# The mixer of a gated decoder step, in another order

## The chip, the cores and the metric

The kernel runs on one core of one Trainium2 chip, as a single launch. The metric is the device time of an execution in microseconds (us). Three runs of the kernel before took 2404.18, 2404.9 and 2407.2 us; the median is 2404.9.

## The reference, cut to what matters

All arithmetic is float32. One layer works on 304 token columns: 16 meta tokens, 256 prompt tokens, and 8 samples of 4 new tokens.

```
x = x + 1/2 * SwiGLU_1(rms(x))
z = rms(x) @ W_in                      # 2048 -> 1024 + 1024 + 2048 + 2048 columns
u_pool, u_ssm, g_a, g_b = z
a = pool_mix(u_pool)                   # window means (2, 4, 8, 16) less u, then a 256x256 map per group, a scale
s = gelu(s5_scan(u_ssm))               # complex diagonal recurrence over the tokens, 64 groups of 64 states
s = s * sigmoid(s @ W_glu + b_glu)
x = x + (sigmoid(g_a + b) * (a @ W_a) + sigmoid(g_b + b) * (s @ W_b)) @ W_out
x = x + 1/2 * SwiGLU_2(rms(x))
y = rms(x)                             # and the new histories and scan states are returned
```

The gates, the branches and everything after them need only the 288 columns without the meta tokens.

## The kernel before, in words

**Layout.** Features lie on the partitions, tokens along the free dimension. Every float32 matrix product is made of three products of float32r parts: high times high, high times low, low times high (`mm3`, L241 to L245).

**Weights.** All weights are read once, in chunks of 512 x 256 (512 KB), in the order that `weight_order` writes out: 698 chunks. For each chunk SP issues a load into one of three `raw` buffers (`load`), ScalarE makes the high part `whi` (L143) and VectorE the low part `wlo` (L152), which frees the raw buffer. Both parts have four buffers and run two chunks ahead of their use. A chunk is 24 matmuls.

**Projections.** `proj` multiplies two column tiles of a weight with the activations, into two of four PSUM banks. After each chunk it calls `step`. A step emits, in this order: the high part of a later chunk, the functions that wait in `g.post` (they read the banks of the projection before), the low part of that chunk, the next load, and then pieces of side work: `g.side` is one generator of which `g.rate` pieces are taken per step on average. The order of the instructions on each engine's queue is that in which they are emitted.

**Mixer.** The first projection `ps0` of the combined input weight is made before `mixer` begins. Then follow, in this order: three more projections for the pool columns, four for the ssm columns, eight times a gate-a projection and a branch-a projection (after the first gate `mixed()` makes the per-group pool maps, on the same four banks), eight gate-b projections, and, once `drain` has emptied the side work, the GLU and branch b.

**Side work.** While the first ssm projections run, the pool branch is the side work, 3.5 pieces per step (`Pool.run`, 40 pieces for four groups; the first piece of a group reads the projection's two banks, L971). At the first ssm projection it is drained, and the scan takes its place after a lag of 7 steps, 2.35 pieces per step. The scan (`Scan.run`) goes through 16 batches. A batch has 12 vector steps (`rows`, L887 to L897, two of them scan instructions), six products with the input (`into`, L835, whose results ScalarE copies) and the products with the output matrix (`outof`, L846). For each batch `load` issues four kinds of DMA on POOL's queue: u, expanded in DRAM (`stk`, 228 KB), the input matrices `bl` (384 KB), the turning factors `ee` (912 KB), and u itself for every other one.

**u of the scan.** `u_in` takes a tile of the ssm columns from its bank, splits it in two parts, stores it once from SP (`usc`) and three times from POOL (`stk`, L1035, 152 KB each).

**Gates.** `gate` multiplies a bank by 1/rms (L1041) and takes the sigmoid; a gates are multiplied with branch a and stored (`msc`), b gates are stored (`gsc`), from SP.

Of the kernel before, what the change touches and what calls it, by code (L numbers as in the profile page):

```python
# [36 lines left out]
MIXRATE = 2.35  # L37
# [5 lines left out]
JB = 2  # L43
NA = S0 // 16
NTV = 16 + NA
POOLRATE = 3.5
LATE = 8
LAG = 7
# [35 lines left out]
def weight_order():  # L84
    """Every weight chunk in the order of use: (array, first row tile, row tiles, first column)."""
    def cols(name, c0, kd):
        return [(name, k0, KC, c0) for k0 in range(0, kd, KC)]

    def ffn_order(i):
        out = []  # L90
        down = lambda c: [(f"ffn{i}_w_down", c * FC, FC, q * 256) for q in range(8)]
        for p in range(NF // 2):
            out += cols(f"ffn{i}_w_gate", p * 256, KD) + cols(f"ffn{i}_w_up", p * 256, KD)
            if p >= 3 and p % 2 == 1:
                out += down((p - 3) // 2)
        return out + down(NF // FC - 1)

    out = ffn_order(1)
    for p in range(KW):
        out += cols("w_in", p * 256, KD)  # L100
    for p in range(KD // 2):
        out += cols("w_in", 2 * WP + p * 256, KD)
        if p == 0:
            out += [("pool_w", 0, 4, 0), ("pool_w", 4, 4, 0)]
        out += cols("w_branch_a", p * 256, KW)
    for p in range(KD // 2):
        out += cols("w_in", 2 * WP + D + p * 256, KD)
    for p in range(KW // 2):
        out += cols("glu_w", p * 256, KW)
    for p in range(KD // 2):  # L110
        out += cols("w_branch_b", p * 256, KW)
    for p in range(KD // 2):
        out += cols("w_out", p * 256, KD)
    return out + ffn_order(2)


class Weights:
    """Brings the chunks in ahead of their use and splits each in two float32r parts."""
# [44 lines left out]
def setup(ctx, tc, I):  # L163
    g = Ctx()
    nc = tc.nc
    g.tc, g.nc, g.I = tc, nc, I
    g.uid = 0
    g.side, g.rate, g.owed, g.post = None, 0, 0.0, []
    g.dram = ctx.enter_context(tc.tile_pool(name="dram", bufs=1, space=DRAM))
    g.const = ctx.enter_context(tc.tile_pool(name="const", bufs=1))  # L170
    g.w = Weights(g, ctx.enter_context(tc.tile_pool(name="wpool", bufs=2)))
    g.act = ctx.enter_context(tc.tile_pool(name="act", bufs=1))
    g.parts = {"X": (g.act, 2 * KD)}
    g.psum = ctx.enter_context(tc.tile_pool(name="psum", bufs=4, space=PSUM))
    g.psaux = ctx.enter_context(tc.tile_pool(name="psaux", bufs=3, space=PSUM))
    g.pslong = ctx.enter_context(tc.tile_pool(name="pslong", bufs=1, space=PSUM))
    g.downs = 0

    g.ident = g.const.tile([P, P], F32, name="ident")
    make_identity(nc, g.ident)  # L180
    g.ones = g.const.tile([P, P], F32, name="ones")
    nc.vector.memset(g.ones, 1.0)
    g.vec = g.const.tile([P, 120], F32, name="vec")
    g.hc = g.const.tile([P, NT + NTV + 2], F32, name="hc")
    g.isc = g.dram.tile([32, JB, NT], F32R, name="isc")
    return g


def load_vectors(g, pool):
    """The per-feature vectors as columns; the first of them is wanted before the others."""  # L190
    nc, I = g.nc, g.I
    vr = pool.tile([P, P], F32, name="vr")
    for name, (r0, n) in VROWS.items():
        src = I[name] if name == "final_norm" else I[name][0]
        nc.gpsimd.dma_start(vr[r0:r0 + n], src.rearrange("(k p) -> k p", p=P))
    nc.gpsimd.dma_start(g.hc, I["consts"])

    def turn(r0, n):
        ps = bank(g, "vt", aux=True)
        nc.tensor.transpose(ps[:, :n], vr[:n], g.ident[:n, :n])  # L200
        nc.vector.tensor_copy(g.vec[:, r0:n], ps[:, r0:n])

    return turn
# [7 lines left out]
def step(g):  # L211
    """Closes a chunk of products: what waits for the chunk before it, then some of the side work."""
    g.w.high()
    flush(g)
    g.w.low()
    g.w.load()
    g.owed += g.rate
    while g.owed >= 1.0:
        g.owed -= 1.0
        got = next(g.side, None) if g.side is not None else None  # L220
        if got is None:
            g.side = None
# [8 lines left out]
def also(g, more):  # L231
    g.side = more if g.side is None else chain(g.side, more)


def drain(g):
    while g.side is not None:
        if next(g.side, None) is None:
            g.side = None
# [9 lines left out]
def warm(g, func):  # L248
    """Has the function's table loaded before it is needed."""
    t = g.act.tile([P, 1], F32, tag="warm", name=nm(g, "warm"))  # L250
    g.nc.scalar.activation(t, g.ones[:, :1], func)
# [11 lines left out]
def split(g, src, n, which, scale=None):  # L263
    """src (times a per-row scale) as two float32r parts whose sum it is."""
# [21 lines left out]
class Norm:  # L286
    """x * gain goes on in two parts; the token's 1/rms is applied to the products (add),
    or to x itself (scaled) once every row tile has been seen by square."""
# [9 lines left out]
    def add(self, xts, squares=True, late=None):  # L298
        """The next row tiles of x; their low parts wait in late if it is given."""
# [35 lines left out]
    def inverse(self):  # L335
        """1/rms of each token as a column of a small tile, from the sums of its squares."""
# [20 lines left out]
    def spread(self):  # L357
        """1/rms of each token in a bank, the same in every row."""
# [11 lines left out]
def rsqrt(g, y, src, shape):  # L370
    """1 / sqrt(src / D + EPS): a guess from the bits, negated, and three Newton steps that each flip it."""
# [14 lines left out]
def load_x(g, tp, norm):  # L386
    """Pieces of the token rows, turned so that features lie on partitions; also their squares' sums."""
# [39 lines left out]
def proj(g, name, c0, xs, n, kd, before=None):  # L427
    """The products of two 128-column tiles of a weight from column c0 on with xs; each in a bank."""
# [14 lines left out]
def ffn(g, pool, norm, i, hpart, done, before=None, last=False):  # L443
    """x += 0.5 * (silu(xn wg) * (xn wu)) wd; done(ms) once row tiles ms of x are whole."""
# [93 lines left out]
def ssm_setup(g):  # L538
    """Everything of the scan that its inputs do not touch; yields between pieces."""
# [261 lines left out]
class Scan:  # L801
    """The groups' states in a frame that turns with them, so that the scan's factors are real."""

    def __init__(self, g, sp, usc, stk):
# [6 lines left out]
        self.yps = {}  # L811
# [3 lines left out]

    def load(self, sb):
        g, sp, nc = self.g, self.sp, self.g.nc
        i, half = divmod(sb, 4 // JB)
        ee = sp.tile([P, 3, JB, NT], F32, tag="ee", name=nm(g, "ee"), bufs=2)
        bl = sp.tile([P, 3 * JB, P], F32R, tag="bl", name=nm(g, "bl"), bufs=1)  # L820
        nc.gpsimd.dma_start(self.stk[sb % 2][:96], self.up[i][half * JB:(half + 1) * JB].rearrange("j r t -> r j t"))
        nc.gpsimd.dma_start(bl, g.bsc[sb])
        nc.gpsimd.dma_start(ee, g.esc[sb])
# [5 lines left out]
    def into(self, sb, s, k):  # L829
        """One of the products with the input that the next batch starts from."""  # L830
# [32 lines left out]
    def rows(self, sb, s):  # L863
        """The batch's work, one vector instruction at a time."""
# [35 lines left out]
    def run(self):  # L900
        nb = NJ // JB
        nxt = self.load(0)
        yield 1
        yield 1
# [39 lines left out]
class Pool:  # L944
    """The pooling branch: each tile's window means less itself, and the new history."""
# [19 lines left out]
    def run(self, p, pss, norm, out):  # L965
        """The group's work, in pieces."""
        g, nc, n = self.g, self.g.nc, NB * HIST
        if norm.r is None:
            norm.finish()
# [46 lines left out]
def mixer(g, norm, O, ps0):  # L1016
    """Gated sum of the two branches; returns its row tiles in two parts."""
# [27 lines left out]
    with ExitStack() as cm:  # L1045
        g.mix = cm.enter_context(g.tc.tile_pool(name="mix", bufs=1))
        with ExitStack() as cs:
# [5 lines left out]
            g.side, g.rate = None, POOLRATE  # L1053
            for p in range(KW // 2):
                pool.fetch(p)
                ps = proj(g, "w_in", p * 256, norm.x, NT, KD) if p else ps0
                more = lambda p=p, ps=ps: also(g, pool.run(p, ps, norm, dparts))
                g.post.append(more if p else lambda more=more: g.post.append(more))
            nc.gpsimd.dma_start(O[3][0, :, :HIST - NS], g.I["state_pool"][0, :, NS:])
            for p in range(KW // 2):  # L1060
                ps = proj(g, "w_in", WP + p * 256, norm.x, NT, KD)
                g.post += [lambda i=2 * p + f, q=ps[f]: u_in(i, q) for f in range(2)]
                if p == 0:
                    drain(g)
                    g.side, g.rate = scan.run(), MIXRATE
                    g.owed = -LAG * MIXRATE
# [17 lines left out]
            for p in range(KD // 2):  # L1084
                pg = proj(g, "w_in", 2 * WP + p * 256, live, NL, KD)
# [12 lines left out]
            for p in range(KD // 2):  # L1098
                pg = proj(g, "w_in", 2 * WP + D + p * 256, live, NL, KD)

                def gated(p=p, pg=pg):
                    for f in range(2):
                        nc.sync.dma_start(gsc[2 * p + f], gate(pg[f], KD + 2 * p + f))

                g.post.append(gated)
# [3 lines left out]
        g.side, g.rate = scan.store(O, mixb), 0.5  # L1109
# [37 lines left out]
def final(g, ctx, O):  # L1147
    """done(ms) for the last layer, and the closing norm."""
# [67 lines left out]
def body(ctx, tc, I, O):  # L1216
# [6 lines left out]
    with ExitStack() as c1:  # L1223
# [37 lines left out]
        def started():  # L1261
            ct.close()
            g.side, g.rate = ssm_setup(g), SETRATE
# [12 lines left out]
        ps0 = proj(g, "w_in", 0, n2.x, NT, KD, lambda c: [late.pop(0)() for _ in range(min(len(late), 2))])  # L1276
# [52 lines left out]
```

## Time and profile before

The profile is of one execution; its span, from the first to the last instruction, is also its own time as the trace gives it. The runs are timed without it.

| | |
|---|---|
| median of three runs | 2404.9 us |
| profiled execution, span | 2402.5 us |
| TensorE busy | 2368.2 us, 99% of the span |
| VectorE busy | 1593.5 us, 66% |
| ScalarE busy | 1013.3 us, 42% |
| DMA, mean | 185 GB/s |
| mixer, from its first projection to the GLU | about 922 to 1365 us of the span |

Reading it: busy times overlap, so the engine with 99% sets the time, and what the other engines do costs something only where TensorE waits for it. TensorE starts matmuls closer together than one lasts, so their durations add up to more than its busy time. The arrow in a name reads "out <- in".

### The profile page before, as it was taken

To read this page: it belongs to the slowest core of one execution; us is meant where nothing else is said; L and a number is where in the kernel's file an instruction comes from. 1 tells how busy PE (TensorE), PEld (TensorE's weight loads), DVE (VectorE), ACT (ScalarE), POOL (GpSimd) and SP (SyncE) were. 2 spreads that over 40 slices of the span, in tenths; PEclk is the share of its full clock that TensorE was granted. 3 is DMA by queue.
4 is the path that set the end of the run, shared out by engine and by line. 5 is a ranking of instruction groups with operands and counts; after the bars stand their busy time and mean duration, and the time that the engine had idled before them with its cause. 6 is when DMAs were issued, how large, how long until landed. Compare 5 with 4: busy or idle time off the path is not lost.

```text
span 2402.5 us, 42577 instructions
## 1 busy us (share of the span) xinstructions
PE 2368.2 (99%) x17321; PEld 2339.4 (97%) x17321; DVE 1593.5 (66%) x2416; ACT 1013.3 (42%) x1617; POOL 137.6 (6%) x233
## 2 busy tenths in 40 slices
PE   8999999999999999979999999999999999999998
PEld 8999999999999999979999999999999999999997
DVE  6788777876655558669988775555555555555555
ACT  5333333344564335344445444433333333333334
POOL 1000000001110002220101031000000000000000
PEclk9999999999999999989999999999999999999999
DMA  6555666666555556697777576555555555555553
GB/s 195 156 154 188 201 200 197 205 202 180 182 178 181 158 159 197 174 252 236 234 233 245 183 246 208 162 167 167 166 167 164 163 167 166 167 166 168 167 167 110
DMA packets 407076, 443.27 MB, mean 185 GB/s; under 512 B 25036, under 2 KB 393904, under 8 KB 406872
## 3 DMA queue, kind: packets, MB, share of 16 engines
q1 hardware_dynamic: 376512, 376.75, 50.5%
q0 software_dynamic: 30368, 63.80, 9.0%
q8 instruction: 136, 2.23, 0.4%
q14 instruction: 60, 0.49, 0.1%
HBM read 404.30 MB, written 36.51 MB: 183 GB/s over the span
## 4 chain that ended last, share of the span: by engine, by line
PE 89%; issue 6%; DMA 2%; DVE 2%; POOL 1%; ACT 1%; SPq 0%; ACTq 0%; POOLq 0%; DVEq 0%
PE pj L243 21%; PE pj L244 21%; PE pj L245 21%; PE dn L243 7%; PE dn L245 7%; PE dn L244 7%; PE yps L846 1%; DVE wlo L152 1%; DMA bl<-bsc 1%; DMA raw<-in_ffn_w_gate 1%; PE bu L835 1%; POOL bd L756 0%; DMA raw<-in_w_branch_a 0%; ACT whi L143 0%; POOL stk L1035 0%
## 5 line engine op out<-in xcount | busy, mean ns | idle before, releaser
L152 DVE TENSOR_TENSOR wlo<-raw,whi 128x1024 fp32r<-128x1024 f32 x698 | 852.6, 1223 | 596.9 <-ACT whi L143 593.0
L143 ACT CAST whi<-raw 128x1024 fp32r<-128x1024 f32 x698 | 732.9, 1051 | 1102.4 <-PE pj L244 626.8
L243 PE MATMUL pj<-X,whi 128*128 128x304 f32 (+1 forms) x2432 | 739.4, 304 | 0.0
L244 PE MATMUL pj<-X,whi 128*128 128x304 f32 (+1 forms) x2432 | 732.8, 301 | 0.0
L245 PE MATMUL pj<-X,wlo 128*128 128x304 f32 (+1 forms) x2432 | 731.9, 301 | 0.2 <-DVE wlo L152 0.2
L244 PE MATMUL pj<-Y,whi 128*128 128x288 f32 x1728 | 510.8, 296 | 0.0
L243 PE MATMUL pj<-Y,whi 128*128 128x288 f32 x1728 | 510.5, 295 | 0.0
L245 PE MATMUL pj<-Y,wlo 128*128 128x288 f32 x1728 | 509.4, 295 | 0.0
L243 PEld LDWEIGHTS pj<-X,whi 128*128 128x128 f32 x2432 | 459.0, 189 | 6.2 <-issue 5.6
L245 PEld LDWEIGHTS pj<-X,wlo 128*128 128x128 f32 x2432 | 460.0, 189 | 0.6 <-DVE wlo L152 0.6
L244 PEld LDWEIGHTS pj<-X,whi 128*128 128x128 f32 x2432 | 460.3, 189 | 0.0
L243 PEld LDWEIGHTS pj<-Y,whi 128*128 128x128 f32 x1728 | 325.9, 189 | 1.5 <-issue 0.9
L244 PEld LDWEIGHTS pj<-Y,whi 128*128 128x128 f32 x1728 | 325.2, 188 | 0.0
L245 PEld LDWEIGHTS pj<-Y,wlo 128*128 128x128 f32 x1728 | 325.2, 188 | 0.0
L243 PE MATMUL dn<-H,whi 128*128 128x304 f32 x704 | 213.8, 304 | 0.2 <-DVE x L481 0.2
L245 PE MATMUL dn<-H,wlo 128*128 128x304 f32 x704 | 213.2, 303 | 0.0
L244 PE MATMUL dn<-H,whi 128*128 128x304 f32 x704 | 212.4, 302 | 0.0
L244 PE MATMUL dn<-X,whi 128*128 128x288 f32 x704 | 208.1, 296 | 0.0
L243 PE MATMUL dn<-X,whi 128*128 128x288 f32 x704 | 208.1, 296 | 0.0
L245 PE MATMUL dn<-X,wlo 128*128 128x288 f32 x704 | 207.9, 295 | 0.0
L243 PEld LDWEIGHTS dn<-X,whi 128*128 128x128 f32 x704 | 132.9, 189 | 0.0
L243 PEld LDWEIGHTS dn<-H,whi 128*128 128x128 f32 x704 | 132.4, 188 | 0.5 <-DVE x L481 0.5
(274 smaller groups left out, 2009.4 us busy)
## 6 DMA issues: line engine op xcount, KB each, us to landing
raw<-in_ffn_w_gate SPq DMA_DIRECT2D x176, 512.0 KB, 3.6
raw<-in_ffn_w_up SPq DMA_DIRECT2D x176, 512.0 KB, 3.6
raw<-in_ffn_w_down SPq DMA_DIRECT2D x176, 512.0 KB, 3.5
raw<-in_w_in SPq DMA_DIRECT2D x96, 512.0 KB, 4.7
raw<-in_w_out SPq DMA_DIRECT2D x32, 512.0 KB, 4.4
esc<-ee POOLq DMA_DIRECT2D x16, 912.0 KB, 5.0
ee<-esc POOLq DMA_DIRECT2D x16, 912.0 KB, 7.5
raw<-in_w_branch_a SPq DMA_DIRECT2D x16, 512.0 KB, 4.4
```

The costliest lines, as they stand in the source:

```text
L143: self.g.nc.scalar.copy(hi, self.raw[i])
L152: self.g.nc.vector.tensor_tensor(lo, raw, hi.bitcast(F32), ALU.subtract)
L243: mm(ps, wh, x[0], start=start, stop=False)
L244: mm(ps, wh, x[1], start=False, stop=False)
L245: mm(ps, wl, x[0], start=False, stop=stop)
L835: self.g.nc.tensor.matmul(ps, s["bl"][:, jj * 3 + ri], self.stk[sb % 2][:, jj], start=True, stop=True)
L846: g.nc.tensor.matmul(self.yps[i][o:o + 32], g.clhs[h][:, sb * JB + jj], s["k"][h][:, jj, NMETA:], start=k == 0, stop=k == 2)
```

## The change

- The order of the projections becomes: ssm columns (the first of them is now `ps0`), pool columns, the eight gate-b projections, then the eight pairs of gate a and branch a, with `mixed()` after the first gate a. `weight_order` follows.
- The single side work becomes a list of `Lane` objects, each with its generator, its rate and what it is owed; a step takes pieces from each of them in turn. The scan's lane is made after the second ssm projection, with 1.5 pieces per step (`MIXRATE0`) after 5 steps of lag. The pool branch has a lane of its own with 1.8 pieces per step, made when the first pool projection is done, and is extended by each of the others. Once it is empty the scan's lane gets 2.25 pieces per step.
- `Scan.__init__` issues the loads of `bl` for batch 0 and of `ee` for batches 0 and 1; `load` issues those that are not there yet. `load(0)` is called where the lane is made.
- `norm.finish` runs in the step before the first `u_in`, not inside the pool's first piece.
- Docstrings are emptied.

```diff
-MIXRATE = 2.35
+MIXRATE = 2.25
+MIXRATE0 = 1.5
-POOLRATE = 3.5
+POOLRATE = 1.8
-LAG = 7
+LAG = 5
...
 def step(g):
     g.w.high()
     flush(g)
     g.w.low()
     g.w.load()
-    g.owed += g.rate
-    while g.owed >= 1.0:
-        g.owed -= 1.0
-        got = next(g.side, None) if g.side is not None else None
-        if got is None:
-            g.side = None
+    for lane in list(g.lanes):
+        lane.go()
...
+class Lane:
+    def __init__(self, g, work, rate, late=0.0):
+        self.g, self.work, self.rate, self.owed = g, work, rate, -late * rate
+        g.lanes.append(self)
+    def also(self, more):
+        self.work = chain(self.work, more)
+    def go(self):
+        self.owed += self.rate
+        while self.owed >= 1.0 and self in self.g.lanes:
+            self.owed -= 1.0
+            self.piece()
+    def piece(self):
+        if next(self.work, None) is None:
+            self.g.lanes.remove(self)
...
 class Scan:
...
+        self.matrices(0)
+        for sb in range(2):
+            self.factors(sb)
...
     def load(self, sb):
-        ee = sp.tile([P, 3, JB, NT], F32, tag="ee", name=nm(g, "ee"), bufs=2)
-        bl = sp.tile([P, 3 * JB, P], F32R, tag="bl", name=nm(g, "bl"), bufs=1)
         nc.gpsimd.dma_start(self.stk[sb % 2][:96], ...)
-        nc.gpsimd.dma_start(bl, g.bsc[sb])
-        nc.gpsimd.dma_start(ee, g.esc[sb])
+        if sb not in self.bl:
+            self.matrices(sb)
+        if sb not in self.ee:
+            self.factors(sb)
+        ee, bl = self.ee.pop(sb), self.bl.pop(sb)
...
 def mixer(g, norm, O, ps0):
...
+            for p in range(KW // 2):
+                ps = proj(g, "w_in", WP + p * 256, norm.x, NT, KD) if p else ps0
+                into = [lambda i=2 * p + f, q=ps[f]: u_in(i, q) for f in range(2)]
+                if p:
+                    g.post += into
+                else:
+                    g.post.append(lambda into=into: g.post.extend([norm.finish] + into))
+                if p == 1:
+                    lane = Lane(g, scan.run(scan.load(0)), MIXRATE0, LAG)
+            means = None
             for p in range(KW // 2):
                 pool.fetch(p)
-                ps = proj(g, "w_in", p * 256, norm.x, NT, KD) if p else ps0
+                ps = proj(g, "w_in", p * 256, norm.x, NT, KD)
+                def pooled(p=p, ps=ps):
+                    nonlocal means
+                    work = pool.run(p, ps, norm, dparts)
+                    if means in g.lanes:
+                        means.also(work)
+                    else:
+                        means = Lane(g, work, POOLRATE)
+                g.post.append(pooled)
...
             for p in range(KD // 2):
+                pg = proj(g, "w_in", 2 * WP + D + p * 256, live, NL, KD)
+                def gated(p=p, pg=pg):
+                    for f in range(2):
+                        nc.sync.dma_start(gsc[2 * p + f], gate(pg[f], KD + 2 * p + f))
+                g.post.append(gated)
+                if means not in g.lanes:
+                    lane.rate = MIXRATE
+            means.drain()
+            for p in range(KD // 2):
                 pg = proj(g, "w_in", 2 * WP + p * 256, live, NL, KD)
...
```

## Rows read from the trace of the kernel before

**Rows 1.** The page, first part: busy us, share of span, count.

```profile
PE 2368.2 (99%) x17321; PEld 2339.4 (97%) x17321; DVE 1593.5 (66%) x2416; ACT 1013.3 (42%) x1617; POOL 137.6 (6%) x233
```

**Rows 2.** Waits of TensorE: us in total, times, longest us.

```profile
PE bu L835 <- DMA bl<-bsc: 10.7, 1, 10.7
...
PE pw L243 <- DVE z L1041: 5.4, 1, 5.4
```

**Rows 3.** Windows: length, busy us by engine (count), granted clock, DMA share, GB/s.

```profile
1033.51:1038.08 4.57, 4.57 (x18) 4.57 (x19) 2.63 (x3) 1.67 (x3) 3.42 (x6) 0.50 0.86 188
...
1067.35:1072.21 4.86, 4.86 (x20) 4.86 (x21) 2.81 (x6) 3.71 (x8) 0.59 (x1) 0.50 0.94 321
...
1083.00:1360.00 277.00, 277.00 (x2008) 257.58 (x2007) 247.32 (x334) 134.40 (x232) 25.23 (x44) 1.00 0.75 231
```

**Rows 4.** POOL timeline: start, us, engine, line, operation, out<-in, count, [idle before <-releaser].

```profile
923.71 1.03 POOL L809 DMA_DIRECT2D stk<-isc  x2
...
995.10 4.10 POOL L1035 DMA_DIRECT2D stk<-Y  x6 [4.10 <-ACT Y L1029]
...
1012.04 4.04 POOL L1035 DMA_DIRECT2D stk<-Y  x6 [12.85 <-ACT Y L1029]
...
1016.73 0.61 POOL L822 DMA_DIRECT2D bl<-bsc  x1
```

**Rows 5.** ScalarE timeline, splits whose weight chunk was late.

```profile
1007.87 1.05 ACT L143 CAST whi<-raw 128x1024 fp32r<-128x1024 f32 x1 [7.59 <-DMA raw<-in_w_in]
...
1028.65 1.04 ACT L143 CAST whi<-raw 128x1024 fp32r<-128x1024 f32 x1 [13.42 <-DMA raw<-in_w_in]
```

**Rows 6.** VectorE timeline, low parts of the weight chunks.

```profile
948.39 1.23 DVE L152 TENSOR_TENSOR wlo<-raw,whi 128x1024 fp32r<-128x1024 f32 x1 [0.49 <-ACT whi L143]
...
1000.31 1.23 DVE L152 TENSOR_TENSOR wlo<-raw,whi 128x1024 fp32r<-128x1024 f32 x1 [1.36 <-ACT whi L143]
...
1013.59 3.49 DVE L152 TENSOR_TENSOR wlo<-raw,whi 128x1024 fp32r<-128x1024 f32 x3
...
1029.72 1.23 DVE L152 TENSOR_TENSOR wlo<-raw,whi 128x1024 fp32r<-128x1024 f32 x1 [12.64 <-ACT whi L143]
```

**Rows 7.** TensorE timeline, a chunk's first (954) or last matmul.

```profile
954.24 0.39 PE L243 MATMUL pj<-X,whi 128*128 128x304 f32 x1
...
1009.09 0.30 PE L245 MATMUL pj<-X,wlo 128*128 128x304 f32 x1
...
1015.79 0.30 PE L245 MATMUL pj<-X,wlo 128*128 128x304 f32 x1
...
1022.52 0.30 PE L245 MATMUL pj<-X,wlo 128*128 128x304 f32 x1
```

**Rows 8.** DMA of 980 to 994 (first row), then of 995 to 1012.

```profile
raw<-in_w_in SPq DMA_DIRECT2D x4, 512.0 KB, 3.6
...
DMA packets 5176, 2.96 MB, mean 174 GB/s; under 512 B 2485, under 2 KB 5175, under 8 KB 5175
...
q1 hardware_dynamic: 2007, 2.00, 37.5%
...
q0 software_dynamic: 3168, 0.94, 35.5%
...
raw<-in_w_in SPq DMA_DIRECT2D x4, 512.0 KB, 10.0
```

**Rows 9.** Windows of 20 us, pool stretch; columns as Rows 3.

```profile
960.00:980.00 20.00, 20.00 (x146) 19.98 (x145) 14.43 (x32) 8.24 (x14) 2.42 (x5) 1.00 0.58 182
```

**Rows 10.** Timelines: a gate projection's last matmul, then VectorE's multiply, two pairs.

```profile
1235.45 0.29 PE L245 MATMUL pj<-X,wlo 128*128 128x288 f32 x1
...
1239.40 0.45 DVE L1041 TENSOR_TENSOR z<-pj,rs_y 128x288 f32<-128x288 f32 x1
...
1261.42 0.30 PE L245 MATMUL pj<-X,wlo 128*128 128x288 f32 x1
...
1261.70 0.45 DVE L1041 TENSOR_TENSOR z<-pj,rs_y 128x288 f32<-128x288 f32 x1
```

More of the change, by code (lines that the diff above doesn't have):

```diff
@@ L98, in weight_order @@
     out = ffn_order(1)
-    for p in range(KW):
-        out += cols("w_in", p * 256, KD)
+    for c0 in (WP, 0):
+        for p in range(KW // 2):
+            out += cols("w_in", c0 + p * 256, KD)
+    for p in range(KD // 2):
+        out += cols("w_in", 2 * WP + D + p * 256, KD)
     for p in range(KD // 2):
@@ L105, in weight_order @@
         out += cols("w_branch_a", p * 256, KW)
-    for p in range(KD // 2):
-        out += cols("w_in", 2 * WP + D + p * 256, KD)
     for p in range(KW // 2):
@@ L167, in setup @@
     g.uid = 0
-    g.side, g.rate, g.owed, g.post = None, 0, 0.0, []
+    g.lanes, g.post = [], []
     g.dram = ctx.enter_context(tc.tile_pool(name="dram", bufs=1, space=DRAM))
@@ L228, in flush, with drain @@
         f()
-def also(g, more):
-    g.side = more if g.side is None else chain(g.side, more)
+class Lane:
[12 more added lines that the diff above has]
+            self.g.lanes.remove(self)
+    def drain(self):
+        while self in self.g.lanes:
+            self.piece()
 def drain(g):
-    while g.side is not None:
-        if next(g.side, None) is None:
-            g.side = None
+    for lane in list(g.lanes):
+        lane.drain()
 def mm3(g, ps, wh, wl, x, start, stop):
@@ L810, in __init__, with factors, matrices @@
         self.sparts = []
-        self.yps = {}
+        self.yps, self.ee, self.bl = {}, {}, {}
+        self.matrices(0)
+        for sb in range(2):
+            self.factors(sb)
     def tile(self, name, bufs):
         return self.sp.tile([P, JB, NT], F32, tag=name, name=nm(self.g, name), bufs=bufs)
+    def factors(self, sb):
+        ee = self.sp.tile([P, 3, JB, NT], F32, tag="ee", name=nm(self.g, "ee"), bufs=2)
+        self.g.nc.gpsimd.dma_start(ee, self.g.esc[sb])
+        self.ee[sb] = ee
+    def matrices(self, sb):
+        bl = self.sp.tile([P, 3 * JB, P], F32R, tag="bl", name=nm(self.g, "bl"), bufs=1)
+        self.g.nc.gpsimd.dma_start(bl, self.g.bsc[sb])
+        self.bl[sb] = bl
     def load(self, sb):
@@ L898, in rows, with run @@
                 states]
-    def run(self):
+    def run(self, first):
         nb = NJ // JB
-        nxt = self.load(0)
-        yield 1
-        yield 1
+        nxt = first
         for k in range(6):
@@ L967, in run @@
         g, nc, n = self.g, self.g.nc, NB * HIST
-        if norm.r is None:
-            norm.finish()
         for u, ps in zip(self.u, pss):
@@ L1052, in mixer @@
             dparts, aparts = [], []
-            g.side, g.rate = None, POOLRATE
+            for p in range(KW // 2):
+                ps = proj(g, "w_in", WP + p * 256, norm.x, NT, KD) if p else ps0
[7 more added lines that the diff above has]
+            means = None
             for p in range(KW // 2):
                 pool.fetch(p)
-                ps = proj(g, "w_in", p * 256, norm.x, NT, KD) if p else ps0
-                more = lambda p=p, ps=ps: also(g, pool.run(p, ps, norm, dparts))
-                g.post.append(more if p else lambda more=more: g.post.append(more))
-            nc.gpsimd.dma_start(O[3][0, :, :HIST - NS], g.I["state_pool"][0, :, NS:])
[L1060 to L1066, printed above, removed]
+                ps = proj(g, "w_in", p * 256, norm.x, NT, KD)
[7 more added lines that the diff above has]
+                g.post.append(pooled)
+            nc.gpsimd.dma_start(O[3][0, :, :HIST - NS], g.I["state_pool"][0, :, NS:])
             def mixed():
@@ L1084, in mixer @@
             for p in range(KD // 2):
+                pg = proj(g, "w_in", 2 * WP + D + p * 256, live, NL, KD)
[6 more added lines that the diff above has]
+            means.drain()
+            for p in range(KD // 2):
                 pg = proj(g, "w_in", 2 * WP + p * 256, live, NL, KD)
@@ L1097, in mixer @@
                 g.post.append(gated)
[L1098 to L1105, printed above, removed]
             flush(g)
@@ L1108, in mixer @@
         mixb = cm.enter_context(g.tc.tile_pool(name="mixb", bufs=1))
-        g.side, g.rate = scan.store(O, mixb), 0.5
+        Lane(g, scan.store(O, mixb), 0.5)
         s2 = []
@@ L1262, in started @@
             ct.close()
-            g.side, g.rate = ssm_setup(g), SETRATE
+            Lane(g, ssm_setup(g), SETRATE)
         late = []
@@ L1275, in body @@
         drain(g)
-        ps0 = proj(g, "w_in", 0, n2.x, NT, KD, lambda c: [late.pop(0)() for _ in range(min(len(late), 2))])
+        ps0 = proj(g, "w_in", WP, n2.x, NT, KD, lambda c: [late.pop(0)() for _ in range(min(len(late), 2))])
         g.post.append(n2.begin)
```

## The prediction, made before the kernel was run

> **What bounds the kernel now.** I began with the page: TensorE is busy for 2368.2 of 2402.5 us [rows 1]. The change neither adds nor removes a matmul, so its time is the same matmuls plus whatever TensorE waits for. Next come TensorE's waits: outside the first microseconds and the last ones, only two are longer than 1 us, and both lie in the mixer: 10.7 us for the scan's matrices `bl`, and 5.4 us in `mixed()`, where a bank is not yet read by the gate's multiply [rows 2]. The windows show what follows each: the granted clock stands at 0.50 (the 1.2 GHz level) for the first 4.57 and 4.86 us of matmuls after them, 18 and 20 matmuls where the full level would have done twice that [rows 3]. At half speed half of that time is lost: 2.3 and 2.4 us. The two places cost 10.7 + 5.4 + 2.3 + 2.4 = 20.8 us. That is all that can be won.
>
> Then the supply behind the first wait. POOL issues six stores of u (`stk`, for two row tiles) in one burst, and in the second burst the first scan loads come right behind them [rows 4]. ScalarE's `whi` then waits for its weight chunk: 7.59 us after the first burst, 13.42 after the second [rows 5]. So the 10.7 us wait hides another. A chunk is 24 matmuls, 3.35 us (two chunks lie between 1009.09 and 1015.79). I call "lead" the time from a chunk's `wlo` being done to TensorE's first matmul on it. Before the first burst it is 1009.1 − 1001.5 = 7.6 us; the second chunk after it has 1015.8 − 1014.8 = 1.0; the fourth, last of the three `wlo` from 1013.59 to 1017.08, has 1022.5 + 0.1 − 1017.1 = 5.5 [rows 6, 7]. A burst thus digs the lead down by 6.6 us and gives back all but 2.1. The next chunk's `wlo` ended at 1030.95; TensorE, had `bl` been there, would have wanted it at 1022.6 + 3.35 = 1026.0. Five of the 10.7 us would have been lost to weights anyway.
>
> **The change, part by part.**
>
> *Scan tables loaded at the start.* `bl` of batch 0 and `ee` of batches 0 and 1 are issued where the `isc` loads stand now, 923.71 [rows 4], some 90 us before their present place. The wait for `bl` goes: −10.7, and −2.3 of clock. What is late next is the load of u itself, `stk`. The first pair of u tiles is stored from about 945, its load follows on POOL when those stores have landed (about 956), and the lane's first product comes six steps after the lane is made (5 of LAG, 1.5 per step), near 970: some 14 us for it, so I count no wait. The early loads are 0.38 + 2 × 0.91 = 2.2 MB beside the weights. The split they could delay stands at 933, and the two adds behind it must be done by 939, when TensorE wants the sum of squares; cost 0, and up to 2 us if that cover goes.
>
> *Ssm columns first.* The four bursts now come in the four projections straight after the norm, without scan loads except one `stk`. Is the DMA then enough? In the stretch of the first burst of before, which has no scan load, q1 moved 2.00 MB in 37.5% of 17 us, so 3.2 us per MB, and q0's 0.94 MB of `stk` took 35.5% of 17 = 6.0 us [rows 8]. Four chunks and two `usc` stores are 2.39 MB: 7.6 us. Together 13.7 us in the 13.4 us of four chunks: just too much, which agrees with the loss of 2.1 us of lead per burst. A weight chunk took 3.6 us to land in the quiet stretch and 10.0 in the burst [rows 8], with three raw buffers. At the new place the first burst begins with less lead: behind the norm's small VectorE chain the `wlo` started at 948.39 ends at 949.6 for a chunk at 954.2, so 4.6 us [rows 6, 7]. First stall 6.6 − 4.6 = 2.0; the three others find the lead spent and cost the 2.1 us by which supply falls behind: 2.0 + 3 × 2.1 = 8.3 us. Bounds: 0, if the lead refills between bursts to the 7.6 of before; 13, if each later burst costs as half again as much with `stk` loads and history loads between (2.0 + 3 × 3.7). I take 8.3, which is nearest to the burst that had no scan loads.
>
> The Trainium skill ("DMA: Bandwidth & Descriptors", Specifications) says that pieces under 512 B do not reach line rate. The 2485 small packets of the burst stretch agree with it: q0's MB took twice q1's [rows 8]. If the `stk` bytes cost what weight bytes do, a burst would take 3.0 us instead of 6.0, the period 10.6 of 13.4, and this term would be nothing: that is the first rival. The bursts keep their shape here, so the rule speaks for the term.
>
> *Pool work in a lane of its own.* Before, 3.5 pieces a step: VectorE was busy for 14.43 of 20 us [rows 9]; with `wlo` at 1.22 per 3.4 us step that leaves (14.43 × 3.4 / 20 − 1.22) / 3.5 = 0.35 us a piece. Scan steps: 247.32 busy of 277 us [rows 3], 73 chunks, so 3.39 per step; less 1.22 and about 0.25 for gates, 1.9 for 2.35 steps, 0.82 each. After, in the pool stretch: 1.22 + 1.5 × 0.82 + 1.8 × 0.35 = 3.1 us per step of about 3.7 (TensorE has the scan's products too). 83%: it holds, as 89% held before, when no TensorE wait stood there. Cost 0.
>
> But a bank is due. The 40 pieces at 1.8 per step start at the first step of pool column 1; the 28th, which reads the last pool column's two banks, comes at the 16th step from there, the last step of the first gate-b projection. The second gate-b projection takes those banks at once. TensorE then waits until VectorE has done that step's work. What that takes is seen where gate multiplies stand behind a whole step's work: they start 0.3 us (1261.42 to 1261.70) to 4.0 us (1235.45 to 1239.40) after the last matmul; these are the ends of the 15 pairs after the first [rows 10]. Plus 0.45 for the read: 0.7 to 4.4; as a value 2.3, a little under the middle, since VectorE is less full there; below, 0.
>
> *b gates before a gates; `mixed()` later.* The wait at `mixed()` was 5.4 because VectorE also stood for a late chunk there. At the new place there is no burst, and the scan has run long since. What is left is the same ordering: the gate's multiply behind a whole step's VectorE work, 0.7 to 4.4 us, against 1.6 us of matmuls (12 at 0.13) that cover it: 0 to 2.8, middle about 1.0, and some 0.7 more for the next two pairs, whose splits go ScalarE then VectorE. I take 1.7 (0.3 to 3.5): −5.4 − 2.4 + 1.7.
>
> *Rates.* 202 scan pieces: 46 by the 36th step of the lane at 1.5, then 70 steps at 2.25, so the last falls in the last step of the a gates, as the last of 204 falls in the last step of the b gates now. Where it ran at 2.35 there were no waits; 2.25 is less. The tail costs 0. The weight order holds the same 698 chunks; the docstrings cost nothing. b gates' stores on SP, ahead of weight loads, are the same sixteen.
>
> **Sum.** 20.8 − 8.3 − 2.3 − 1.7 = 8.5 us gained: span 2402.5 → 2394.0. The median of runs is 2404.9, 2.4 us around the span: 2396.4 us predicted. Its own range, 2390 to 2400.
>
> **Rivals.**
>
> *All is won.* The bursts find lead enough and the banks come in time: 20.8 less at most 3: 2384 to 2387. For it: the loads that made the second burst so bad (`bl`, `ee`) are gone from it, and before burst 1 there was 7.6 us. Against: 13.7 of 13.4 us of DMA, and only 4.6 us at the start. 25%.
>
> *Slower, through the clock.* Both waits of before were followed by the 1.2 GHz level, and the trace has no idle stretch between 1 and 5 us to tell what a short one does. If each of the six new short waits (four bursts, a bank, `mixed()`) is followed by a half-clock stretch as those were, 2.35 us each, then 14.1 is lost: 2396.4 + 14.1 = 2410.5. It decides at the length of wait from which the level falls; the waits I expect are 2 to 2.5 us. For it: two out of two. Against: those were twice as long and more. 12%.
>
> *The wait only changes its name.* The first product stands for `stk` instead of `bl`, or weights starve for the 13 us of the upper bound: 20.8 − 13 − 4 = 4, so about 2401, within the noise. 13%.
>
> **How the numbers follow.** My forecast has 50%. 0.2% is 4.8 us, about what measurement can tell here: the bounds are 2400.1 and 2409.7. Faster: nearly all of the forecast (45) and the full gain (25): 70%. Same: the rest of the forecast, the third rival and a little of the clock: 19%. Slower: 11%. Range: from the full gain, 2385, to 2406, between the third rival and the clock's.
>
> **What would show it.** In the profile after: no TensorE wait on `bl`; `whi` waiting for weights near 958, 973, 988 with TensorE idle for about 2 us at `wlo` each time; a TensorE wait on `pt L971` at the second gate-b projection; one under 3 us in `mixed()`; granted clock 1.00 through the mixer. I am wrong if TensorE has no `wlo` waits after 945 (all is won), if the clock is 0.50 in several stretches, or if a wait on `stk` appears.

## The result, and the profile after

The changed kernel takes 2409.1 us (median of 17 runs, 2406.3 to 2416.6), the kernel before 2404.2 beside it (17 runs, 2400.7 to 2408.7): ratio 1.002, 95% interval 1.0013 to 1.0027. It is slower by 0.2%, where I forecast 2396.4. The profiled execution's span is 2409.9 us.

TensorE's waits in the changed kernel (us in total, times, longest us), which answer to [rows 2]:

```profile
PE bu L868 <- DMA bl<-bsc: 6.1, 1, 6.1
...
PE pj L263 <- DVE wlo L154: 5.0, 4, 3.4
PE pj L261 <- ACT whi L145: 2.9, 1, 2.9
PE ss L361 <- DVE acc L350: 2.3, 2, 1.7
PE pj L261 <- DVE pt L1000: 2.3, 1, 2.3
PE pj L261 <- DVE Y L290: 1.1, 1, 1.1
PE pw L261 <- DVE z L1070: 0.3, 1, 0.3
```

The two long waits of before have become many. In the mixer TensorE idles 6.1 (`bl`, again), 5.0 + 2.9 (weights), 1.7 (sum of squares; the other 0.6 is at the very end), 2.3 (banks of the pool) and 1.4 (`mixed()` and the first branch a): 19.4 us against 16.1.

The windows in which the clock stood lower, columns as in [rows 3]:

```profile
967.99:971.40 3.41, 3.41 (x15) 3.41 (x15) 0.93 (x1) 0.00 (x0) 0.00 (x0) 0.50 0.83 115
...
998.71:1002.12 3.41, 3.41 (x16) 3.41 (x15) 2.51 (x5) 2.44 (x6) 2.81 (x5) 0.50 0.78 228
...
1019.50:1022.60 3.10, 3.10 (x12) 3.10 (x13) 2.40 (x5) 0.85 (x3) 0.00 (x0) 0.50 0.59 190
...
1077.21:1080.62 3.41, 3.24 (x13) 3.27 (x14) 2.91 (x6) 2.25 (x5) 0.00 (x0) 0.50 0.49 165
```

Four stretches, 13.3 us at half speed, 6.7 us lost, where the kernel before lost 4.7. They stand behind the two longest weight waits, the wait for `bl` and the pool's; behind the 1.7 us for the sum of squares the clock stayed. Idle and clock together: 26.1 us against 20.8, so 5.3 more. The medians differ by 4.9, the two profiled spans by 7.5. Of these 0.5 stands before the second chunk already; 1.7 us I cannot place.

ScalarE's splits that waited for a weight chunk, as in [rows 5]:

```profile
961.12 1.05 ACT L145 CAST whi<-raw 128x1024 fp32r<-128x1024 f32 x1 [9.93 <-DMA raw<-in_w_in]
...
976.79 1.05 ACT L145 CAST whi<-raw 128x1024 fp32r<-128x1024 f32 x1 [9.89 <-DMA raw<-in_w_in]
...
995.81 1.04 ACT L145 CAST whi<-raw 128x1024 fp32r<-128x1024 f32 x1 [11.11 <-DMA raw<-in_w_in]
...
1014.43 1.04 ACT L145 CAST whi<-raw 128x1024 fp32r<-128x1024 f32 x1 [10.60 <-DMA raw<-in_w_in]
```

One for each store burst, as forecast. (`stk<-Y` is a store of u, `stk<-stk` the load that reads u back.) The wait for `bl` is that of the second batch. It has one buffer, so it can be loaded only when the first batch's products are made, and its issue stands on POOL right behind the fourth burst (POOL, then TensorE; compare [rows 4]):

```profile
999.31 4.20 POOL L1064 DMA_DIRECT2D stk<-Y  x6 [13.99 <-ACT Y L1058]
1003.50 0.68 POOL L851 DMA_DIRECT2D stk<-stk  x1
1004.15 0.61 POOL L845 DMA_DIRECT2D bl<-bsc  x1
...
1019.48 0.59 PE L868 MATMUL bu<-stk,bl 128*128 128x304 f32 x1 [6.13 <-DMA bl<-bsc]
```

It took 15 us to land. Before, the first batch's `bl` stood just so behind the second burst.

### The profile page after: what moved, and what is told of

It is laid out like the page before. It is cut to its first block, busy times and chain, and to the rows that moved or that the text cites. A ratio compares the mean times of both kernels' runs of the same rounds, so it can differ in the third digit from the quotient of the medians.

```text
span 2409.9 us, 42569 instructions
## 1 busy us (share of the span) xinstructions
PE 2372.5 (98%) x17321; PEld 2341.8 (97%) x17321; DVE 1592.1 (66%) x2416; ACT 1012.9 (42%) x1617; POOL 138.0 (6%) x233
## 2 busy tenths in 40 slices
DMA packets 407076, 443.27 MB, mean 184 GB/s; under 512 B 25036, under 2 KB 393904, under 8 KB 406872
## 4 chain that ended last, share of the span: by engine, by line
PE 86%; issue 7%; DMA 3%; DVE 2%; POOL 1%; ACT 1%; ACTq 0%; SPq 0%; POOLq 0%; DVEq 0%
PE pj L261 21%; PE pj L262 21%; PE pj L263 21%; PE dn L261 7%; PE dn L263 7%; PE dn L262 7%; PE yps L879 1%; DMA raw<-in_w_in 1%; DVE wlo L154 1%; DMA bl<-bsc 1%; DMA raw<-in_ffn_w_gate 1%; PE bu L868 0%; ACT whi L145 0%; POOL bd L774 0%; POOL stk L1064 0%
```

## The experiments

Theory A: the stores of u starve everything that is loaded beside them, the weights and the scan's tables, in the old place and in the new. Theory B: tables and weights are simply too many bytes, and `bl` has one buffer.

**x2: u into tiles of 128 rows, twice.** Each store of u goes to a tile of its own with 128 rows; the high part, wanted twice, is stored once and read twice.

```diff
-        stk = g.dram.tile([4, 96, NT], F32R, name=nm(g, "stk"))
-        for k, x in enumerate((hi, lo, hi)):
-            nc.gpsimd.dma_start(stk[:, k * 32:(k + 1) * 32], x)
+        stk = [g.dram.tile([P, NT], F32R, name=nm(g, "stk")) for _ in range(2)]
+        for s, x in zip(stk, (hi, lo)):
+            nc.gpsimd.dma_start(s, x)
...
-        nc.gpsimd.dma_start(self.stk[sb % 2][:96], self.up[i][half * JB:(half + 1) * JB].rearrange("j r t -> r j t"))
+        for k, x in enumerate((0, 1, 0)):
+            src = self.up[i][x][half * JB * 32:(half + 1) * JB * 32].rearrange("(j r) t -> r j t", j=JB)
+            nc.gpsimd.dma_start(self.stk[sb % 2][k * 32:(k + 1) * 32], src)
```

> The changed kernel, with u of the scan stored twice per tile (high and low part) as whole rows of 1216 B into tiles of 128 rows, where the changed kernel stores it three times in pieces; the scan reads it back with three loads per batch in place of one. Theory A, store bursts: the stores in small pieces starve the weight loads and hold up the second batch's bl, which is issued behind the fourth burst. Then the waits of TensorE for wlo and whi between 960 and 1000 us (7.9 us idle, 3.4 us of half clock) go, the bl wait (6.1 + 1.6) falls below 1 us, and the time is 17 to 20 us under the changed kernel's 2409: about 2390, ratio to before 0.994. Theory B, table loads and bytes: stores do not matter, the DMA is short of bytes and bl has one buffer; the saving is at most 3 us: 2406 to 2409, ratio about 1.001.

Measured: 2388.9 us, ratio to before 0.9922 (0.9907 to 0.9937). Every TensorE wait on `bl` is gone, the one wait for weights that is left is short, and the clock is 1.00 through the whole mixer:

```profile
PE pj L263 <- DVE wlo L154: 0.4, 1, 0.4
```

Theory A holds. Its saving was put too low: by the two ratios x2 is some 23 us under the changed kernel (the profiled spans say 22.7), where 17 to 20 were foretold.

**x7: u into tiles of 128 rows, three times.** The same, with the high part stored twice as well. Bytes and number of stores are those of the changed kernel; as in x2, u is read back with three loads per batch in place of one.

> The changed kernel with three stores of u per tile, as it has them, but each as 128 whole rows of 1216 B into a tile of its own; the scan reads them back with three loads per batch. Bytes and number of stores are those of the changed kernel, only the pieces differ. If the size of the pieces is the cause: a burst costs about 3 us of all 16 engines in place of 6, the starvation is gone as in x2, ratio to before 0.992 to 0.994, 2387 to 2392. If the bytes are the cause (x2 stored a third less): the starvation is back, ratio 1.000 to 1.002.

Measured: 2390.0, ratio 0.9938 (0.9925 to 0.9952). The layout of u is the cause, not the bytes. (The split of the loads was not tried by itself.) The changed kernel's DMA, then that of x7 (packets; the stores, with their median us to landing):

```profile
DMA packets 407076, 443.27 MB, mean 184 GB/s; under 512 B 25036, under 2 KB 393904, under 8 KB 406872
...
stk<-Y POOLq DMA_DIRECT2D x24, 152.0 KB, 10.7
```

```profile
DMA packets 398372, 443.23 MB, mean 186 GB/s; under 512 B 16332, under 2 KB 385200, under 8 KB 398168
...
stk<-Y POOLq DMA_DIRECT2D x24, 152.0 KB, 4.0
```

24 stores of the same 152 KB took 4.0 us to land in place of 10.7. But the size of the pieces is not what changed, though my expectation says so. Packets of 512 B and more are as many in both kernels (407076 − 25036 and 398372 − 16332, 382040 each), and the 8704 packets under 512 B that x7 saves make 0.04 MB, so about 4 bytes each. The packets in the trace say the same: both kernels store u and read it back in 6144 packets of 1216 B, whole rows. A store into a tile whose first dimension is 4 puts 400 packets of 4 bytes beside its 128 rows, a store into 128 rows only 16; the six stores of [rows 8] are 6 × 528 = 3168 packets.

What did change is how fast the rows move. Two stretches inside the first burst, the changed kernel from 952 to 954, x7 from 952 to 953.5 (q0 is POOL's queue, q1 that of the weights):

```profile
DMA packets 621, 0.22 MB, mean 109 GB/s; under 512 B 442, under 2 KB 621, under 8 KB 621
...
q0 software_dynamic: 616, 0.21, 73.9%
q1 hardware_dynamic: 5, 0.00, 0.8%
```

```profile
DMA packets 407, 0.45 MB, mean 300 GB/s; under 512 B 37, under 2 KB 407, under 8 KB 407
...
q0 software_dynamic: 405, 0.45, 116.5%
q1 hardware_dynamic: 2, 0.00, 0.2%
```

In both the weights get next to nothing, but in the changed kernel POOL's queue moves 0.21 MB in 2 us, in x7 0.45 MB in 1.5 (there the first loads of u are in it). And in the changed kernel the 16 engines were only 75% busy meanwhile. (Packets overlap in the records, so a share can pass 100%.) Whether the 4-byte packets or the slower rows hold the weights back was not separated: that the layout is the cause is shown, by which of the two it acts is not. Around the whole first burst q0 held the engines for 46.0% of 16 us in the changed kernel and 40.7% of 13 us in x7, 7.4 and 5.3 us for 1.25 and 1.26 MB:

```profile
q0 software_dynamic: 3374, 1.25, 46.0%
...
raw<-in_w_in SPq DMA_DIRECT2D x3, 512.0 KB, 10.2
```

```profile
q0 software_dynamic: 1127, 1.26, 40.7%
...
raw<-in_w_in SPq DMA_DIRECT2D x3, 512.0 KB, 8.0
```

(The changed kernel from 948 to 964, then x7 from 947 to 960.) That is 2.1 us less, not the 3 I had worked out, and the weights land only 2 us sooner. It was enough: TensorE has no weight wait in x7 at all.

**x5: the kernel before, with x2's stores.**

> The kernel before, with u stored as in x2: twice per tile, whole rows, three loads per batch. Theory A: the stores delay bl and the weights in the old order too, so the 10.7 us wait for bl falls to 0 to 3 us and the wait in mixed() to about 2: 13 to 18 us under before, 2386 to 2391. Theory B: the first scan loads are late because ee and bl are large and issued late; the wait for bl falls by no more than 3 us: 2400 to 2404.

Measured: 2390.6, ratio 0.9929 (0.9915 to 0.9942). The wait for `bl`, 10.7 us, is gone without touching when or how the tables are loaded; in `mixed()` 2.5 is left:

```profile
PE pw L243 <- DVE z L1043: 2.5, 1, 2.5
```

So the old order suffered from the same stores, and the new one paid for them in another place.

**x1: two buffers for `bl`**, both loaded at the start (`bufs=2`, `self.matrices(1)`).

> The changed kernel, with two buffers for bl and the bl of batches 0 and 1 both loaded at the start; nothing else. Theory A: the 6.1 us wait for bl goes, but the same burst delays the weights, whose split at 1016.7 belongs to a chunk that would then be wanted at 1013.2, so some 3.5 us stay at the same place under another name, and 384 KB more at the start lengthen the wait for the sum of squares by up to 1 us: 2405 to 2408. Theory B: the whole 6.1 us and the 1.6 us of half clock behind it go: 2401.

Measured: 2413.8, ratio 1.0025 (1.0016 to 1.0034), no better than the change (1.0020) and above both forecasts. Two of its waits:

```profile
PE bu L869 <- DMA stk<-stk: 5.3, 1, 5.3
...
PE ss L361 <- DVE acc L350: 3.0, 2, 2.3
```

The place and nearly the whole of the wait stayed, under the name of u's load, which stood in the same queue. I had expected the weights there, 3.5 us. And the sum of squares waits 2.3 us in place of 1.7, with 384 KB more loaded at the start.

**x4: without the early loads** (the three lines in `Scan.__init__` taken out; `load` issues all).

> The changed kernel without its early loads: bl and ee of the first batches are issued by the scan's own load, where the lane is made. The early loads' own cost goes: the 1.7 us wait for the sum of squares at 939 falls to 0 to 0.5. If they were worth their place: the first product waits for bl again, 3 us or more, since 1.3 MB then land among the first two store bursts, and the time is 2412 or more. If not (my theory: the first product comes only 6 steps after the lane is made, which is cover enough): no wait on the first product, weights starve 2 to 4 us more in the second burst, 2408 to 2412, ratio 1.001 to 1.003.

Measured: 2407.2, ratio 1.0006 (0.9997 to 1.0015). The first product waits for nothing; the second batch's waits for `bl` as before, 6.2 us; the wait for the sum of squares is 0 inside the mixer. My expectation that the weights would starve 2 to 4 us more was wrong: TensorE waits 5.2 us for them in this profile, where the changed kernel has 7.9. So the early loads bought nothing that the profile shows and cost the wait for the sum of squares, behind which the clock fell to 0.50 for 3.4 us in the profiles of x1, x3 and x7. That this moves the time is not shown: the interval overlaps the changed kernel's (1.0013 to 1.0027).

**x3: 2.0 pool pieces per step.**

> The changed kernel, with 2.0 pool pieces per step in place of 1.8, so that the piece that reads the last pool projection's banks comes one step before TensorE wants them. Theory C: the 2.3 us wait on the pool's multiply at 1075 goes, and the half clock behind it (1.7): 2405. Rival: VectorE is full in that stretch, wlo comes late instead and the time stays at 2409 or rises.

Measured: 2408.7, ratio 1.0008 (0.9999 to 1.0018). The bank wait is gone and VectorE kept up: no `wlo` wait after 1000. That this moves the time is not shown, since the interval overlaps the change's; the wait for `bl` was 7.0 in its profile.

**x8 and x9: x2 without the early loads, and that with 2.0 pool pieces.**

> x2 (u stored twice per tile as whole rows) without the early loads of bl and ee. Theory: with the bursts light the late loads land in time, no TensorE wait on bl, the wait for the sum of squares (1.4 us in x2) goes: 1 to 2 us under x2, ratio 0.9915. Rival, early loading pays: a wait on bl or ee of 3 us or more, ratio 0.9935.

> x8 with 2.0 pool pieces per step: the bank wait of 0.6 us that x2 keeps goes. 0.5 us under x8 if VectorE keeps up, ratio 0.991 to 0.992; if VectorE falls behind, wlo waits appear between 1000 and 1050 us and it is 1 us or more over x8.

Measured: x8 2391.7, ratio 0.9947 (0.9935 to 0.9960); x9 2387.6, ratio 0.9933 (0.9921 to 0.9946). In x8 the wait for the sum of squares is gone, but the bank wait has grown to 2.1 us with 3.4 us of half clock behind it, so it did not come under x2. x9 has neither; its longest wait in the mixer:

```profile
PE pj L261 <- DVE Y L290: 1.1, 1, 1.1
```

**x9 and x5 again, side by side.**

> x9 once more, beside x5 on one chip, to tell what the new order is worth with the stores in whole rows. TensorE idles 1.8 us in the mixer of x9 (no half clock), 4.9 us in that of x5 with 1.7 us lost to half clock: 4 to 5 us between them, x9 2386 to 2388, ratio about 0.992.

> x5 once more, beside x9: 2390 to 2392, ratio about 0.994. If it comes within 1 us of x9, the order with its lanes is worth nothing that can be measured.

Measured: x9 2389.7, ratio 0.9936 (0.9924 to 0.9949); x5 2389.4, ratio 0.9933 (0.9920 to 0.9946). My 4 to 5 us are not there, though the profiled spans (2385.7 and 2388.7) lean that way. With the stores into tiles of 128 rows the new order is worth nothing that these runs can tell. Both beat the kernel before by 0.65%, and the changed kernel by a little more.

**c1 and c2: what a short wait costs in clock.** Twenty pauses in the second FFN of x9; one run each, 2478.4 and 2477.8 us, read for their traces alone.

```diff
+def pause(g, n):
+    ps = bank(g, "pz", aux=True)
+    t = g.act.tile([P, NT], F32, tag="gw", name=nm(g, "pz"))
+    g.nc.tensor.matmul(ps[:, :NL], g.ident, g.x[0][:, NMETA:], start=True, stop=True)
+    g.nc.scalar.copy(t[:, :NL], ps[:, :NL])
+    for _ in range(n - 1):
+        g.nc.scalar.copy(t[:, :NL], t[:, :NL])
+    g.nc.tensor.matmul(ps[:, :2], t[:, :P], g.ones[:, :2], start=True, stop=True)
```

> x9, and in the second FFN, where TensorE otherwise never waits, 20 pauses some 35 us apart: one product, n copies on ScalarE one after the other, one product that waits for them; n is 1, 1, 2, 2, up to 10, 10. Idle stretches of about 1 to 5.5 us. If short waits cost the clock (what the profile of the changed kernel suggests: falls after 1.9 us and more, none after 0.7 and less): the granted clock falls to 0.50 after most pauses from about 2 us, for 3.4 us or more each, and each costs 1.7 us beside itself. If only waits as long as those of the kernel before do (my forecast): falls only from 5 us on, at the last two.

> The same 20 pauses in falling order, n from 10 to 1, so that each length stands at other times. The same as c1 is expected by each theory; where the two differ for one length, the length alone does not decide.

Measured, over both: how many of the idle stretches of each length were followed by a granted clock of 0.50.

| idle, us | 0.49 | 0.95 | 1.41 | 1.88 | 2.34 | 2.80 | 3.26 | 3.73 | 4.19 | 4.65 |
|---|---|---|---|---|---|---|---|---|---|---|
| pauses followed by a fall | 0 of 4 | 0 of 4 | 0 of 4 | 1 of 4 | 3 of 4 | 3 of 4 | 4 of 4 | 4 of 4 | 4 of 4 | 4 of 4 |

Two pauses of the same length in c1, TensorE's rows, and the windows behind them:

```profile
1784.24 0.39 PE L468 MATMUL pz<-ones,pz 128*128 128x2 f32 x2 [1.88 <-ACT pz L467]
...
1839.65 0.39 PE L468 MATMUL pz<-ones,pz 128*128 128x2 f32 x2 [1.87 <-ACT pz L467]
```

```profile
1784.70:1788.10 3.40, 3.40 (x16) 3.40 (x16) 1.23 (x1) 1.11 (x3) 0.00 (x0) 0.50 0.18 47
1839.70:1843.10 3.40, 3.40 (x26) 3.40 (x27) 1.22 (x1) 1.53 (x3) 0.00 (x0) 1.00 0.05 13
```

Read the counts: 16 matmuls at 0.50, 26 at 1.00 in the same 3.4 us. Between 1.88 and 2.80 us the length alone does not decide; up to 1.41 none fell, from 3.26 all did. My forecast's 5 us is wrong.

## Why the prediction was wrong

The order of working was right: TensorE's waits, their clock, and what would be late next. Of the terms:

- *20.8 us to win.* Borne out: x2 won 18.0 (2406.9 before beside it, 2388.9), x5 16.4, and no run more than 20.8.
- *Weights starving in the four bursts, 8.3 us.* Measured 7.9 idle. That the stores starve the weights is right (x2, x7); that the size came out is part luck. By burst TensorE idled 3.4, 0.9, 3.6 and nothing, where I had 2.0 and three times 2.1; in the fourth the late weights are hidden behind the wait for `bl`. The working under it does not hold either. 13.7 us in 13.4 makes 0.3 us a burst, not 2.1, and the engines were 75% busy while the weights got next to nothing. And I took the 2485 packets under 512 B for pieces of u, where they are packets of 4 bytes beside whole rows. So the Trainium skill's sentence on pieces under 512 B ("DMA: Bandwidth & Descriptors", Specifications) does not bear on these stores. (The upper bound has a slip: half as much again as 2.1 is 3.2, which gives 11.5 us, not 13.)
- *Banks of the last pool projection, 2.3 us.* Measured 2.3, at the second gate-b projection, on `pt`: the place was worked out, the exact figure is chance, a value from within 0.7 to 4.4.
- *`mixed()`, 1.7 us.* Measured 1.4 (0.3 and 1.1).
- *Early loads, cost 0, "up to 2 us if that cover goes".* It went: the split that should have stood at 933 waited for its chunk until 938 and TensorE 1.7 us for the sum of squares. 2.2 MB at once ahead of it were too much: x4, without them, has no such wait.
- *"The wait for `bl` goes: −10.7 ... so I count no wait."* **This is the step that failed first.** The first batch's wait did go. But I followed the first batch's loads and stopped there. The second batch's `bl`, with one buffer, is issued in the one burst that I had not looked behind, the fourth, and TensorE waited for it just as it had for the first batch's: 6.1 us, and 1.6 of half clock behind it. And x1 shows that it would not have helped to see `bl` alone, since u's load waits there too. I had the fact in hand, that stores make everything land late, and applied it to the weights only.
- *No clock loss after short waits.* **The second step that failed**, and as large: 6.7 us, of which 5.1 behind the waits for weights and the pool's banks. I had put it at nothing in the sum and gave it 12% on the ground that the two waits of before were longer. The pauses show that more than half of those between 1.9 and 2.8 us fall (7 of 12).

Put together: 12.3 us forecast, +6.1 for `bl`, +1.7 for the sum of squares, +6.7 for the clock, −0.7 for the other three, gives the 26.1 that the profile shows. Neither failed step alone (7.7 and 5.1 us) uses up the 8.5 us that I had forecast as gain; both together do. The second rival's mechanism took part, and so did the third's. That the second's 2410.5 lies so near the measured time is luck: it had 14.1 us of clock and no wait for `bl`.

Where the gain went, then: the change moved the stores of u to a place where the weights have less lead, and kept their layout. Most of what it removed as one wait came back as several, and behind four of these the clock fell as well.

## What to carry to other kernels

When a wait for a load is removed, ask what made the load slow before asking when it was issued: here ten changed lines in the layout of a scratch store were worth 16 to 18 us in either order, and the order of four stages nothing that can be told. Before calling packets small, ask how many bytes they carry: thousands of packets under 512 B made 0.04 MB here. Follow every round of a repeated load through a new order, not the first alone, and the other loads of its queue with it. Several short waits of TensorE are not cheaper than one long one of the same sum, since each of 2 us or more can cost the clock.

## What the hardware showed that I had not expected

- A store from 128 partitions into a scratch tile of first dimension 4 landed in 10.7 us, into a tile of 128 rows in 4.0 (medians of 24, x7). Both moved whole rows of 1216 B; the first came with 400 packets of 4 bytes, the second with 16. The Trainium skill ("DMA: Bandwidth & Descriptors", Rules for kernel authors) says that an outermost dimension below 16 confines a transfer to at most that many engines, here four. The trace does not name the engine of a packet, but it fits: while the first store of a burst was alone (949.4 to 949.8), 3.8 of its rows were under way at a time on average, and 19.6 in x7 (950.6 to 951.0). The rule's advice, to put the 128 rows outermost, is what x7 bears out.
- The granted clock fell after one of four idle stretches of 1.88 us and after all sixteen from 3.26 us; each fall showed 3.4 us at 0.50, in five of these sixteen 6.8.
